# Starting the FFN behind each mixer on x times its modulation, with the RMS root applied to the products

## The chip, the cores and the metric

The kernel runs on one core of a Trainium2 chip. The metric is the device time of one execution in microseconds (us): the median of several runs. The profile is of one further execution on the chip, and its times count from the start of its span.

The engines are named as in the profile: PE (matmuls; PEld its weight loads), DVE, ACT, POOL (GpSimd) and SP. Each works through its own queue in order and waits at semaphores for the others.

## The reference

Two layers, 256 latent tokens and 256 context tokens, 1024 channels. Layer 0 mixes tokens by a 2-D Fourier transform, layer 1 by retention. A half-step FFN stands ahead of and behind each mixer, and each of them begins with an RMS norm and a modulation.

```
def rmsnorm(x, g):
    y = x * rsqrt(mean(x * x, axis=-1) + NORM_EPS)
    return y * g

def modulate(h, shift, scale):
    return h * (1 + scale) + shift

def swiglu(h, w_gate, w_up, w_down):                    # FFN_DIM = 2816
    return (silu(h @ w_gate) * (h @ w_up)) @ w_down

for l in range(2):
    def half_ffn(t, m, j):
        h = modulate(rmsnorm(t, norm_g[l, j]), m[3 * j], m[3 * j + 1])
        return t + 0.5 * m[3 * j + 2] * swiglu(h, w_gate[l, j // 2], w_up[l, j // 2], w_down[l, j // 2])
    x = half_ffn(x, m_lat, 0)
    ctx = half_ffn(ctx, m_ctx, 0)
    y_lat, y_ctx = fourier_layer(...) if l == 0 else retention_layer(...)
    x = x + m_lat[5] * y_lat                            # and ctx likewise, in layer 0
    x = half_ffn(x, m_lat, 2)                           # and ctx likewise, in layer 0
return rmsnorm(x, final_g)
```

The root of the norm is one number for each token. A matmul with the weights therefore commutes with it: W applied to (x · scale · root + shift) is (W applied to x · scale) · root + W applied to shift, with the root along the tokens and the last term one number for each output channel.

## The kernel before

Activations lie transposed: channels on the 128 partitions (eight tiles, d or k = 0 to 7), tokens in the free dimension, 256 latent columns first and 256 context columns behind them. `xlat` and `xctx` are the residual streams.

**Products.** An fp32 product is made of three fp32r matmuls (`mm3`): high part by high part (L132), high weight by the activation's low part (L133), low weight by the high part (L134). A weight block arrives raw by SP's DMA queue; ACT rounds its high part (L89, `wh`), DVE subtracts to get the low part (L90, `wl`), in pieces of 128x1024. The activations are split the same way: `h` tiles come in pairs, high and low.

**The FFN.** The 2816 hidden channels are 22 blocks of 128, each with a gate and an up product over the eight tiles k; `hidden` then applies Silu (ACT), multiplies (DVE) and splits the result. Block b needs two pieces of weights. The first blocks of each FFN are issued by a special beginning, `begin_two` (512 columns: the latent columns of two blocks first, then their context columns) or `begin_narrow` (256 columns; in the last FFN only the latent stream is left).

**Between a mixer and the FFN.** The mixer's output projection ends per tile d in a residual on DVE (`residual`, L395) and a square on ACT (L307); the squares are added up over d by POOL or DVE (`square`, L314). The last two squares of each stream are left apart (`apart=2`), so that PE sums three tiles. `rstd` then sums over the partitions with PE (L329, one column for each 128 tokens), takes the root (ACT L334, DVE L336), spreads it to a diagonal (L338) and to a row on all partitions (PE L345). `norm_mod` makes the `h` tiles: DVE x · scale · row (L361), ACT the shift and the high part (L362), DVE the low part (L363). Only then can the FFN's first product run. In the meantime `keep_warm` issues matmuls of a constant (L250) whose result nobody uses: 6, 5 and 5 of them.

This happens twice: behind Fourier (`prepare(0, 2, T2, True)`, then `begin_two`) and behind retention (`prepare(1, 2, S, True)`, then `begin_narrow`). The context's norm (`late`) is made while PE multiplies the first latent blocks. `nxt["done"]` holds the norm's operations, and `behind(d)` puts what is issued in it behind the norm of tile d.

**Order.** Each engine's order is set when the kernel is built, by a scheduler that simulates the program; `tc.issue_after` only adds an edge to it. SP's queue of weight loads runs ahead as far as its buffers go (three raw tiles, six pairs of pieces).

In Fourier, `rstd_tokens` computes the root of the mixer's own norm in another form: sums over the partitions for both streams (L384), root (L389) and reciprocal (L391) with tokens on the partitions. DVE and ACT use it in the first Fourier stages.

Of the kernel before, what the change touches and what calls it, by code (L numbers as in the profile page):

```python
# [10 lines left out]
F32 = mybir.dt.float32  # L11
# [5 lines left out]
P = 128  # L17
# [14 lines left out]
GRID_W = 64  # L32


@with_exitstack
def hybrid_block(ctx: ExitStack, tc: tile.TileContext, a: dict, out: bass.AP):
# [44 lines left out]
    def h_tile():  # L81
        return hpool.tile([P, 512], F32R, tag="h", name=nm("h"))
# [176 lines left out]
    sums = {}  # L259

# [43 lines left out]
    def square(d, s, eng=nc.gpsimd, apart=0):  # L304

        sq = q_tile()
        nc.scalar.activation(sq, x_tile(d, s), AF.Square)  # L307
# [45 lines left out]
    def norm_mod(l, j, s, h, r):  # L353
        sl = STREAMS[s]
        done, acts = [], []
        for d in range(ND):
# [3 lines left out]
            with tc.issue_after(done[d - 3].ins) if d > 2 else nullcontext():  # L360
                nc.vector.scalar_tensor_tensor(u, x_tile(d, s), sc, r, ALU.mult, ALU.mult)  # L361
# [16 lines left out]
    def rstd_tokens():  # L378

        ps = aux_tile()  # L380
        for s in range(2):
# [6 lines left out]
        root = spool.tile([P, 4], F32, tag="root4", bufs=1, name=nm("root"))  # L388
        mark[2] = nc.scalar.activation(root, ps[:, :4], AF.Sqrt, bias=epst[:, 1:2])  # L389
        inv = spool.tile([P, 4], F32, tag="inv4", bufs=1, name=nm("inv"))  # L390
# [64 lines left out]
    def half_ffn(l, j, h, width, begin, after, each=None):  # L455
        f = 2 * l + j // 2
        off = 0
        for c0, c1 in CHUNKS:
            hid = []

            def hidden(psg, psu):
                sg = t_tile()
                mark[1] = nc.scalar.activation(sg[:, :width], psg[:, :width], AF.Silu)  # L463
                hf = t_tile()
                nc.vector.tensor_tensor(hf[:, :width], psu[:, :width], sg[:, :width], ALU.mult)  # L465
                uh, ul = a_tile(), a_tile()
                split(uh[:, :width], ul[:, :width], hf[:, :width])
                hid.append((uh, ul))
# [124 lines left out]
    def fourier(l, slot, after):  # L593
# [84 lines left out]
        four["last"] = mark[0], mark[6]  # L678

        for b in range(4):  # L680
# [5 lines left out]
            for d in (2 * b, 2 * b + 1):  # L686
# [49 lines left out]
    def retention(l, slot, h, mid, after):  # L736
# [220 lines left out]
        def project_out(hd, zt, between=None, behind=None):  # L957
            for half in range(2):
                blk = wblock(a["ret_out"][slot, hd, half], 2048)
                for dd in range(4):  # L960
# [7 lines left out]
                    if hd == HEADS - 1:  # L968
                        square(d, 0, nc.vector, 2)
# [4 lines left out]
        for hd in range(HEADS):  # L974
# [55 lines left out]
    def prepare(l, j, width, warm=False):  # L1030
# [16 lines left out]
        return after  # L1047

# [96 lines left out]
    def begin_narrow(load, bank, part, hidden):  # L1145
# [134 lines left out]
```

## Time and profile before

| | us |
|---|---|
| runs | 1652.84, 1654.86, 1654.74 |
| median | 1654.74 |
| profiled execution | 1655.55 |
| its span | 1653.7 |
| Fourier's output projection ends on PE | 439.76 |
| first product of FFN (0,2) | 446.81 |
| retention's output projection ends on PE | 1447.61 |
| first product of FFN (1,2) | 1453.66 |

The profiled execution lies 0.81 us above the median. The timeline lists each engine's instructions with their start and duration; instructions alike that follow each other are drawn together (x4), and what ended an idle time stands in brackets. A window's row gives its length, then each engine's busy time in it, the clock granted to PE as a share of full speed, and the DMA engines' share. A duration in the timeline includes the time in which an instruction drains, so that the next may start before it ends; what one costs in a row of them is the distance between starts.

### The profile page before, as it was taken

What the parts mean: (1) busy time and instruction counts of PE and PEld (TensorE: products, weight loads), DVE (VectorE), ACT (ScalarE), POOL (GpSimd) and SP (SyncE); (2) the same over time, 40 slices, a digit from 0 to 9 for tenths busy, and PEclk for the clock granted to TensorE, in tenths of its full rate; (3) what the DMA queues carried; (4) which work ended last, traced back from release to release, by engine and by line L of the source; (5) the groups of instructions that cost most, each with busy time, mean ns of one, the idle gap of its engine ahead of it and who ended that gap; (6) DMA issues with size and microseconds to landing.
All of it is one profiled execution on the core that took longest, in us unless ns stands there. A gap on an engine that the chain in (4) does not pass through costs nothing.

```text
span 1653.7 us, 23197 instructions
## 1 busy us (share of the span) xinstructions
PE 1632.7 (99%) x9310; PEld 1427.1 (86%) x9310; DVE 1128.3 (68%) x1813; ACT 624.3 (38%) x912; POOL 123.6 (7%) x194
## 2 busy tenths in 40 slices
PE   7999999999999999999999999999999999999998
PEld 5888888888988888888988888888988999999998
DVE  5688888887866776766567767733666757665554
ACT  4422322346543122233442232223564454354443
POOL 0010111113200000001200000001100000000000
PEclk9999999999999999999999999999999999999999
DMA  9675776752244544544144444522133333345451
GB/s 370 225 265 183 265 259 221 252 188 77 77 142 177 178 164 165 192 158 175 52 165 170 166 164 156 191 88 100 63 128 128 128 119 137 129 169 187 166 190 53
DMA packets 59516, 272.03 MB, mean 164 GB/s; under 512 B 7409, under 2 KB 8705, under 8 KB 41745
## 3 DMA queue, kind: packets, MB, share of 16 engines
q1 hardware_dynamic: 40224, 201.76, 34.5%
q0 software_dynamic: 18640, 68.26, 11.7%
q8 instruction: 73, 1.20, 0.3%
q10 hardware_dynamic: 544, 0.52, 0.1%
q14 instruction: 35, 0.28, 0.0%
HBM read 265.27 MB, written 5.24 MB: 164 GB/s over the span
## 4 chain that ended last, share of the span: by engine, by line
PE 96%; DVE 2%; ACT 1%; issue 0%; DMA 0%; DVEq 0%; ACTq 0%
PE ps L132 31%; PE ps L133 31%; PE ps L134 31%; PE ps L790 0%; PE aux L195 0%; PE aux L250 0%; PE aux L329 0%; DVE t L269 0%; PE aux L345 0%; PE aux L951 0%; PE ps L865 0%; DVE a L90 0%; DVE xlat L395 0%; ACT wh L89 0%; DVE a L628 0%
## 5 line engine op out<-in xcount | busy, mean ns | idle before, releaser
L89 ACT CAST wh<-raw 128x1024 fp32r<-128x1024 f32 x344 | 352.3, 1031 | 709.6 <-PE ps L133 608.5
L133 PE MATMUL ps<-h,wh 128*128 128x512 f32 (+1 forms) x1568 | 556.0, 356 | 0.5 <-DVE h L1081 0.5
L134 PE MATMUL ps<-h,wl 128*128 128x512 f32 (+1 forms) x1568 | 554.8, 355 | 0.0
L132 PE MATMUL ps<-h,wh 128*128 128x512 f32 (+1 forms) x1568 | 549.3, 357 | 3.4 <-ACT h L1080 3.1
L90 DVE TENSOR_TENSOR wl<-raw,wh 128x1024 fp32r<-128x1024 f32 x344 | 410.3, 1198 | 179.2 <-ACT wh L89 176.0
L132 PEld LDWEIGHTS ps<-h,wh 128*128 128x128 f32 x1568 | 294.3, 190 | 46.1 <-ACT h L1080 4.0
L133 PEld LDWEIGHTS ps<-h,wh 128*128 128x128 f32 x1568 | 297.1, 190 | 42.6 <-DVE h L1081 1.0
L134 PEld LDWEIGHTS ps<-h,wl 128*128 128x128 f32 x1568 | 296.9, 190 | 41.6 <-DVE wl L90 0.3
L222 DVE CUSTOM_DVE_ANT_0 dump<-araw,wide,adab 128x1024 bf16<-128x1024 f32 x256 | 329.7, 1288 | 3.2
L132 PE MATMUL ps<-a,wh 128*128 128x512 f32 (+2 forms) x952 | 317.8, 337 | 0.0
L134 PE MATMUL ps<-a,wl 128*128 128x512 f32 (+2 forms) x952 | 317.7, 336 | 0.0
L133 PE MATMUL ps<-a,wh 128*128 128x512 f32 (+2 forms) x952 | 317.6, 336 | 0.0
L133 PEld LDWEIGHTS ps<-a,wh 128*128 128x128 f32 x952 | 180.9, 190 | 18.7
L134 PEld LDWEIGHTS ps<-a,wl 128*128 128x128 f32 x952 | 180.8, 190 | 18.4
L132 PEld LDWEIGHTS ps<-a,wh 128*128 128x128 f32 x952 | 180.0, 190 | 18.5
L465 DVE TENSOR_TENSOR t<-ps,t 128x512 f32<-128x512 f32 (+1 forms) x88 | 55.0, 625 | 171.3 <-PE ps L134 140.7
L213 POOL DMA_DIRECT2D araw<-in_ada_w x128 | 67.8, 530 | 819.3 <-DVE mods L222 760.1
L395 DVE SCALAR_TENSOR_TENSOR xlat<-ps,mods,xlat 128x256 f32<-128x256 f32 x128 | 61.1, 481 | 63.5 <-PE ps L134 62.9
L463 ACT ACTIVATE t<-ps 128x512 f32<-128x512 f32 (+1 forms) x88 | 47.9, 544 | 127.9 <-PE ps L134 122.5
L90 DVE TENSOR_TENSOR a<-t,a 128x512 fp32r<-128x512 f32 (+2 forms) x116 | 70.0, 607 | 2.6 <-ACT a L89 2.2
L89 ACT CAST a<-t 128x512 fp32r<-128x512 f32 (+2 forms) x116 | 64.3, 558 | 14.0 <-DVE t L894 9.8
L314 POOL TENSOR_TENSOR q<-q,q 128x256 f32<-128x256 f32 x52 | 47.1, 922 | 178.8 <-ACT q L307 178.3
(216 smaller groups left out, 1150.0 us busy)
## 6 DMA issues: line engine op xcount, KB each, us to landing
raw<-in_wgu SPq DMA_DIRECT2D x85, 1024.0 KB, 4.8
araw<-in_ada_w POOLq DMA_DIRECT2D x128, 512.0 KB, 3.8
raw<-in_wd SPq DMA_DIRECT2D x32, 896.0 KB, 4.5
raw<-in_ret_in SPq DMA_DIRECT2D x24, 1024.0 KB, 4.8
raw<-in_wd SPq DMA_DIRECT2D x16, 1024.0 KB, 4.8
a<-in_ada_first SPq DMA_DIRECT2D x32, 256.0 KB, 6.0
t<-in_four_w SPq DMA_DIRECT2D x32, 256.0 KB, 5.1
raw<-in_ret_out SPq DMA_DIRECT2D x8, 1024.0 KB, 4.7
```

Source lines behind the costliest of these rows:

```text
L89: mark[6] = nc.scalar.copy(hi, src)
L90: i = (lo_eng or nc.vector).tensor_tensor(lo, src, f32(hi), ALU.subtract)
L132: nc.tensor.matmul(ps, lh, rh, start=start, stop=False)
L133: nc.tensor.matmul(ps, lh, rl, start=False, stop=False)
L134: mark[4] = nc.tensor.matmul(ps, ll, rh, start=False, stop=stop)
L213: nc.gpsimd.dma_start(raw, a["ada_w"][l, m, d])
L222: nc.vector.tensor_tensor_reduce(dump, raw, wide[:, v, :], 1.0, adab[:, l, m, d : d + 1], ALU.mult, ALU.add, mods[l][:, m, d, v : v + 1],)
L314: eng.tensor_tensor(n, sums[s][0], sq, ALU.add)
L395: mark[0] = nc.vector.scalar_tensor_tensor(x_tile(d, s), ps, mods[l][:, m, d, s : s + 1], x_tile(d, s), ALU.mult, ALU.add)
L463: mark[1] = nc.scalar.activation(sg[:, :width], psg[:, :width], AF.Silu)
L465: nc.vector.tensor_tensor(hf[:, :width], psu[:, :width], sg[:, :width], ALU.mult)
```

## The change

Both transitions use a new class `Ahead`. Per tile d, right behind the latent residual, `tile(d)` makes the `h` pair from x · scale alone: ACT the high part, DVE the low part. `open` has written the shift (high and low part) into the first two of the context's columns of the `h` tiles, with POOL. The first products run over 258 columns: 256 of x · scale and two of the shift. They are two blocks in `begin_two`, three in `begin_narrow`. The root is computed inside the stream of products (`roots`, at k = 5 or 4), and `evict` multiplies it into the products as they leave PSUM; the shift's product is added per channel, as ACT's bias for the gate and in DVE's multiplication for up. The context's norm later overwrites the shift's columns, and the latent norm (`norm_mod`) is still made, for the blocks that follow. No `keep_warm` is left at the two places.

The squares behind Fourier are all added by POOL, for all eight tiles; those behind retention too, instead of by DVE. Block 1's weights (and block 2's in `begin_narrow`) are cast and split behind tile 7. `rstd_tokens` gets the number of streams and goes through them in reverse; Fourier's own root uses it as well.

```
-    def rstd_tokens():
+    def rstd_tokens(n=2, scale=1.0):
         ps = aux_tile()
-        for s in range(2):
+        for s in reversed(range(n)):
             for t in range(2):
                 for i, sq in enumerate(sums[s]):
                     mark[5] = nc.tensor.matmul(
...
     def fourier(l, slot, following):
...
+        following.open()
         for b in range(4):
...
                 for s in range(2):
                     residual(d, z[:, STREAMS[s]], l, 5, s)
-                    square(d, s, nc.gpsimd, 2)
-                    if d == ND - 1 and s == 0:
-                        sqrt_table()
-                        keep_warm(NW[0], mark[4])
-                        after(0)
-        after(1)
+                    if s == 0:
+                        following.tile(d)
+                for s in (1, 0):
+                    square(d, s)
+        sqrt_table()
...
     def project_out(hd, zt, between=None, behind=None):
...
                     if hd == HEADS - 1:
-                        square(d, 0, nc.vector, 2)
+                        following.tile(d)
+                        square(d, 0)
...
+        following.open()
         project_out(HEADS - 1, zts.pop(0))
-        keep_warm(NW[0], mark[4])
-        after(0)
...
+    class Ahead:
+        def open(self):
+            need(self.l, 3 * self.j + 1)
+            nxt["h"] = self.h = h_tiles()
+            nxt["done"] = [], []
+            for d, (hi, lo) in enumerate(self.h):
+                sh = mods[self.l][:, 3 * self.j, d, 0:1].broadcast_to([P, SH])
+                hi, lo = (t[:, S : S + SH] for t in (hi, lo))
+                nc.gpsimd.tensor_copy(hi, sh)
+                nc.gpsimd.tensor_tensor(lo, sh, f32(hi), ALU.subtract)
+        def tile(self, d):
+            sc = mods[self.l][:, 3 * self.j + 1, d, 0:1]
+            hi, lo = (t[:, STREAMS[0]] for t in self.h[d])
+            nxt["done"][1].append(nc.scalar.activation(hi, x_tile(d, 0), AF.Copy, scale=sc))
+            mark[0] = nc.vector.scalar_tensor_tensor(lo, x_tile(d, 0), sc, f32(hi), ALU.mult, ALU.subtract)
+            nxt["done"][0].append(mark[0])
+        def products(self, blk, ps, k):
+            hi, lo = (t[:, : S + SH] for t in self.h[k])
+            for gu in range(2):
+                mm3(ps[gu][:, : S + SH], wcols(blk, k // 4 * 1024 + gu * 512 + k % 4 * P, P), (hi, lo), k == 0, k == ND - 1)
+        def evict(self, ps, r):
+            col = spool.tile([P, 2], F32, tag="col", name=nm("col"))
+            v = []
+            for gu in range(2):
+                nc.vector.tensor_copy(col[:, gu : gu + 1], ps[gu][:, S : S + 1])
+                v.append(q_tile())
+                nc.vector.tensor_tensor(v[gu], ps[gu][:, :S], r, ALU.mult)
+            return v, col
+        def gate(self, v, col, pair):
+            uh, ul = pair
+            sg = q_tile()
+            mark[1] = nc.scalar.activation(sg, v[0], AF.Silu, bias=col[:, 0:1])
+            hf = q_tile()
+            nc.vector.scalar_tensor_tensor(hf, v[1], col[:, 1:2], sg, ALU.add, ALU.mult)
+            split(uh[:, :S], ul[:, :S], hf)
+        def roots(self, n):
+            inv = rstd_tokens(n, 1.0 / D**2)
+            diag = t_tile()[:, : n * S]
+            nc.vector.tensor_tensor(...)
+            r = aux_tile()
+            for s in range(n):
+                self.rowed = nc.tensor.matmul(r[:, STREAMS[s]], meanw, diag[:, STREAMS[s]], start=True, stop=True)
+            row = q_tile()
+            nc.scalar.copy(row, r[:, :S])
+            return r, row
+        def begin_two(self, load, bank, part, hidden):
+            late = STREAMS[1]
+            h = self.h
+            blks, lat = [load(0)], [(bank(), bank()) for _ in range(2)]
+            with behind(ND - 1), tc.issue_after(squared[0].ins):
+                blks.append(load(1))
+            for k in range(ND):
+                self.products(blks[0], lat[0], k)
+                if k == 5:
+                    r, row = self.roots(2)
+            for k in range(ND):
+                with tc.issue_after(self.rowed.ins) if k > 3 else nullcontext():
+                    self.products(blks[1], lat[1], k)
+            nxt["done"] = norm_mod(self.l, self.j, 1, h, r[:, late])
+            with behind(3):
+                first = self.evict(lat[0], row)
+            with behind(ND - 1):
+                second = self.evict(lat[1], row)
+                pre = [load(2)]
...
+            for k in range(ND):
+                for i in range(2):
+                    for gu in range(2):
+                        part(blks[i], ctx[i][gu], gu, (k,), late)
+                if k == 0:
+                    with tc.issue_after(mark[0].ins), tc.issue_after(mark[6].ins):
+                        nxt["done"] = norm_mod(self.l, self.j, 0, h, r[:, :S])
...
```

`begin_narrow` is written in the same way, with three blocks, one stream and the latent norm into other tiles than those that the first products read.

In the new program the lines move: L90 becomes L94, L132 to L134 become L136 to L138, L314 becomes L319, L361 to L363 become L366 to L368, L384 becomes L389, L395 becomes L400, L702 to L704 become L710 to L712. New are L1077 (ACT) and L1078 (DVE) in `tile`, L1094 and L1096 in `evict`.

What stands in the engines' queues shows three places. The first is PE in the first stage of Fourier, where the sums for its own root are issued among the stage's products (`aux_3459` is the tile of sums, `q_3398` the latent's and `q_3405` the context's sum of squares). Before:

```order
L132 MATMUL ps_3480<-a_2979,h_158 128x256
L384 MATMUL aux_3459<-meanw,q_3398 128x1 x2
L133 MATMUL ps_3480<-a_2980,h_158 128x256
L134 MATMUL ps_3480<-a_2979,h_159 128x256
L132 MATMUL ps_3480<-a_2979,h_156 128x256
L384 MATMUL aux_3459<-meanw,q_3405 128x1 x2
L133 MATMUL ps_3480<-a_2980,h_156 128x256
```

And in the changed program:

```order
L136 MATMUL ps_3480<-a_2979,h_156 128x256
L137 MATMUL ps_3480<-a_2980,h_156 128x256
L138 MATMUL ps_3480<-a_2979,h_157 128x256
L136 MATMUL ps_3480<-a_2979,h_158 128x256
L137 MATMUL ps_3480<-a_2980,h_158 128x256
L389 MATMUL aux_3459<-meanw,q_3405 128x1 x2
L389 MATMUL aux_3459<-meanw,q_3398 128x1 x2
L138 MATMUL ps_3480<-a_2979,h_159 128x256
```

Both sums now stand together, the latent's behind the context's, and the last of them has four products more ahead of it than before.

The second is DVE at the end of Fourier's output projection (`t` are a tile's outputs of both streams, `h` the pairs of the next FFN, `wl` the weights' low parts of its block 1). Before, the rows from the last tile's output on:

```order
L702 TENSOR_TENSOR t_4081<-ps_4052,t_4066 128x2x128
L703 TENSOR_TENSOR t_4081<-ps_4052,t_4066 128x2x128
L704 COPY t_4081<-ps_4052 128x2
L395 SCALAR_TENSOR_TENSOR xlat<-t_4081,mods_126,xlat 128x256
L395 SCALAR_TENSOR_TENSOR xctx_98<-t_4081,mods_126,xctx_98 128x256
L336 RECIPROCAL inv_4122<-root_4120 128x2
L338 TENSOR_TENSOR q_4124<-ident,inv_4122 128x256
```

And in the changed program:

```order
L400 SCALAR_TENSOR_TENSOR xlat<-t_4131,mods_126,xlat 128x256
L400 SCALAR_TENSOR_TENSOR xctx_98<-t_4131,mods_126,xctx_98 128x256
L1078 SCALAR_TENSOR_TENSOR h_3752<-xlat,mods_126,h_3751 128x256
L1078 SCALAR_TENSOR_TENSOR h_3754<-xlat,mods_126,h_3753 128x256
L94 TENSOR_TENSOR wl_4166<-raw_4163,wh_4165 128x1024
L94 TENSOR_TENSOR wl_4170<-raw_4163,wh_4169 128x1024
L396 RECIPROCAL inv_4216<-root_4214 128x4
L1111 TENSOR_TENSOR t_4218<-ident,inv_4216 128x512
```

The low parts of tiles 6 and 7 stand behind every residual, and a pair of weight splits stands ahead of the root's reciprocal.

The third is PE in the new stream, from the last products of block 0 (`wh_4155`, k = 7) to the first of block 1 (`wh_4165`, k = 0); `q_4141` and `q_4145` are the sums of squares, each the result of the last addition for its stream:

```order
L137 MATMUL ps_4160<-h_3754,wh_4155 128x258
L138 MATMUL ps_4160<-h_3753,wl_4156 128x258
L389 MATMUL aux_4209<-meanw,q_4141 128x1 x2
L136 MATMUL ps_4161<-h_3739,wh_4165 128x258
L137 MATMUL ps_4161<-h_3740,wh_4165 128x258
L136 MATMUL ps_4162<-h_3739,wh_4165 128x258
L137 MATMUL ps_4162<-h_3740,wh_4165 128x258
L389 MATMUL aux_4209<-meanw,q_4145 128x1 x2
L138 MATMUL ps_4161<-h_3739,wl_4166 128x258
```

The sums that began the norm before now follow all of block 0's products, and the first product with block 1's low part follows the second sum.

More of the change, by code (lines that the diff above doesn't have):

```diff
@@ L734, in rsqrt_small, with retention @@
         return y
-    def retention(l, slot, h, mid, after):
+    def retention(l, slot, h, mid, following):
         need(l, NMOD - 1)
@@ L1047, in prepare, with __init__, begin_narrow @@
         return after
+    class Ahead:
+        def __init__(self, l, j):
+            self.l, self.j = l, j
+        def open(self):
[16 more added lines that the diff above has]
+            for gu in range(2):
+                mm3(
+                    ps[gu][:, : S + SH], wcols(blk, k // 4 * 1024 + gu * 512 + k % 4 * P, P), (hi, lo),
+                    k == 0, k == ND - 1,
+                )
+        def evict(self, ps, r):
[16 more added lines that the diff above has]
+            diag = t_tile()[:, : n * S]
+            nc.vector.tensor_tensor(
+                diag.rearrange("p (a b) -> p a b", b=P), ident.unsqueeze(1).broadcast_to([P, 2 * n, P]),
+                inv.unsqueeze(2).broadcast_to([P, 2 * n, P]), ALU.mult,
+            )
+            r = aux_tile()
[23 more added lines that the diff above has]
+                pre = [load(2)]
+            ctx = [(bank(), bank()) for _ in range(2)]
+            for k in range(ND):
[5 more added lines that the diff above has]
+                        nxt["done"] = norm_mod(self.l, self.j, 0, h, r[:, :S])
+            pairs = [(a_tile(), a_tile()) for _ in range(2)]
+            with behind(ND - 1):
+                self.gate(*first, pairs[0])
+                self.gate(*second, pairs[1])
+                for i in range(2):
+                    hidden(*ctx[i], pairs[i], late)
+                pre.append(load(3))
+            return 2, pre
+        def begin_narrow(self, load, bank, part, hidden):
+            n = 3
+            blks, lat = [load(0)], [(bank(), bank()) for _ in range(n)]
+            with behind(ND - 1), tc.issue_after(squared[0].ins):
+                blks += [load(i) for i in range(1, n)]
+            for k in range(ND):
+                self.products(blks[0], lat[0], k)
+                if k == 4:
+                    r, row = self.roots(1)
+            first = self.evict(lat[0], row)
+            self.h, h = self.h[:], self.h
+            h[:] = [halves_of(a_tile()) for _ in range(ND)]
+            with tc.issue_after(mark[0].ins), tc.issue_after(mark[6].ins):
+                nxt["done"] = norm_mod(self.l, self.j, 0, h, r[:, :S], slice(0, S), range(5))
+            with behind(4):
+                pre = [load(n)]
+            with tc.issue_after(mark[0].ins), tc.issue_after(mark[6].ins):
+                done = norm_mod(self.l, self.j, 0, h, r[:, :S], slice(0, S), range(5, ND))
+            nxt["done"] = tuple(i + j for i, j in zip(nxt["done"], done))
+            for i in range(1, n):
+                for k in range(ND):
+                    with tc.issue_after(self.rowed.ins) if k > 3 else nullcontext():
+                        self.products(blks[i], lat[i], k)
+            with behind(ND - 1):
+                pre.append(load(n + 1))
+                for ready in [first] + [self.evict(ps, row) for ps in lat[1:]]:
+                    pair = halves_of(a_tile())
+                    self.gate(*ready, pair)
+                    hidden(None, None, pair, None)
+            return n, pre
```

60 lines of the change are left out of this document (28 added, 32 removed).

## The prediction

> **What bounds the kernel now.** I read the page first: its busy times, and the chain that ended last.
>
> ```profile
> span 1653.7 us, 23197 instructions
> PE 1632.7 (99%) x9310; PEld 1427.1 (86%) x9310; DVE 1128.3 (68%) x1813; ACT 624.3 (38%) x912; POOL 123.6 (7%) x194
> PE 96%; DVE 2%; ACT 1%; issue 0%; DMA 0%; DVEq 0%; ACTq 0%
> ```
>
> PE carries the chain nearly throughout. But busy is not useful: 32 of its matmuls at each of two places only keep it occupied while other engines compute a norm. So the second view is PE's timeline at these places (start, duration, instruction, idle time ahead). The first, between Fourier projection and FFN, I call T1:
>
> ```profile
> 439.52 0.28 PE L133 MATMUL ps<-a,wh 128*128 128x258 f32 x1
> 439.64 0.28 PE L134 MATMUL ps<-a,wl 128*128 128x258 f32 x1
> 439.76 1.50 PE L250 MATMUL aux<-meanw 128*128 128x128 f32 x12
> ...
> 445.93 1.02 PE L329 MATMUL aux<-meanw,q 128*128 128x1 f32 x8
> 446.81 0.49 PE L132 MATMUL ps<-h,wh 128*128 128x256 f32 x2
> 447.14 0.28 PE L133 MATMUL ps<-h,wh 128*128 128x256 f32 x1
> 447.26 0.28 PE L134 MATMUL ps<-h,wl 128*128 128x256 f32 x1
> ```
>
> From 439.76 to 446.81 no product of the FFN runs: **7.05 us**. The first two products then take 0.33 us instead of 0.24, a loss of 0.09. The rows also give the price of a product: starts lie 0.12 us apart with 258 columns (439.52, 439.64) and with 256 (447.14, 447.26). T2, behind retention:
>
> ```profile
> 1447.49 0.28 PE L134 MATMUL ps<-a,wl 128*128 128x256 f32 x1
> 1447.61 1.50 PE L250 MATMUL aux<-meanw 128*128 128x128 f32 x12
> 1449.30 1.47 PE L329 MATMUL aux<-meanw,q 128*128 128x1 f32 x12 [0.19 <-DVE q L314]
> ...
> 1453.66 0.74 PE L132 MATMUL ps<-h,wh 128*128 128x256 f32 x4
> ...
> 1455.12 0.52 PE L132 MATMUL ps<-h,wh 128*128 128x256 f32 x3
> ```
>
> From 1447.61 to 1453.66: **6.05 us**. Ten products then take 1.46 us instead of 1.20: 0.26 more.
>
> **The change part by part: what it removes.** The first products now need only x times its scale, so PE can go from the last projection product into the FFN. What remains of the norm on PE stands inside the product stream. Its price there is in the chain of waits (time on the chain, count; each fp32 matmul is recorded twice):
>
> ```profile
> 449.46 0.34 PE aux L329 x4
> 453.50 0.43 PE aux L345 x2
> ```
>
> At T1 the context's last sum (0.34) and row (0.43) stood in the stream already. Now there are four sums (x8: 0.68) and two rows (0.86), 1.54 against 0.77. At T2 there are two sums and one row, 0.77 against nothing outside the gap. Removed: T1 7.05 + 0.09 + 0.77 − 1.54 = 6.37; T2 6.05 + 0.26 − 0.77 = 5.54; **together 11.91 us**. Two more columns cost nothing by the 0.12 pitch; at most 2/256 of 11.5 us of products at T1 and 17.3 at T2, 0.2 us.
>
> **What it adds at T1.** DVE gets eight operations L1078 between the residuals, two of them behind all residuals in the order above. GpSimd gets four more squares' additions (14 instead of 10). Both meet at this stage:
>
> ```profile
> 429.03 2.35 DVE L90 TENSOR_TENSOR wl<-raw,wh 128x1024 fp32r<-128x1024 f32 x2
> 432.02 0.93 DVE L395 SCALAR_TENSOR_TENSOR xlat<-t,mods,xlat 128x256 f32<-128x256 f32 x1
> 432.88 0.96 DVE L395 SCALAR_TENSOR_TENSOR xctx<-t,mods,xctx 128x256 f32<-128x256 f32 x1
> ...
> 438.12 0.41 DVE L702 TENSOR_TENSOR t<-ps,t 128x256 f32<-128x256 f32 x1
> 438.45 0.41 DVE L703 TENSOR_TENSOR t<-ps,t 128x256 f32<-128x256 f32 x1
> ...
> 441.17 0.49 DVE L395 SCALAR_TENSOR_TENSOR xlat<-t,mods,xlat 128x256 f32<-128x256 f32 x1
> 441.57 0.48 DVE L395 SCALAR_TENSOR_TENSOR xctx<-t,mods,xctx 128x256 f32<-128x256 f32 x1
> 429.51 6.51 POOL L314 TENSOR_TENSOR q<-q,q 128x256 f32<-128x256 f32 x6 [35.63 <-ACT q L307]
> 436.28 3.31 POOL L314 TENSOR_TENSOR q<-q,q 128x256 f32<-128x256 f32 x4 [0.27 <-ACT q L307]
> 432.00:442.00 10.00, 10.00 (x86) 9.96 (x85) 9.70 (x21) 4.42 (x12) 7.21 (x9) 1.00 0.30 105
> ```
>
> While GpSimd adds, a DVE operation with two SBUF inputs starts 0.86 us after the one before (432.02, 432.88); alone 0.40 (441.17, 441.57). So each addition puts about 0.47 us into DVE's queue. The last row (busy PE, PEld, DVE, ACT, POOL in ten us) leaves DVE 0.3 us idle; ACT at 4.42 has room for eight more scalings.
>
> The last residual before ends at 441.57 + 0.40 = 441.97. Eight L1078 at 0.395 add 3.2, four additions 1.9; idle time gives back 0.3, and the last two additions fall behind tile 7, onto the weight split (−0.9). Tile 7 is then ready at about 445.8; PE wants it at 439.76 + 42 × 0.12 = 444.80. It waits about 1.1 us for tiles 6 and 7, and some 0.4 more for the last addition's sum. **T1's stalls: 1.5 us.** Below, no contention gives 0 (445.1 less the idle time). Above, an operation that always costs 0.86 puts tile 7 at 449 (rival B). I take the middle because the additions are counted there.
>
> Block 1's split of the weights waits behind tile 7. Behind it on DVE stand the root, the context's norm, the evictions, block 2's split, the latent norm:
>
> ```profile
> 451.50 2.36 DVE L90 TENSOR_TENSOR wl<-raw,wh 128x1024 fp32r<-128x1024 f32 x2
> 453.97 1.26 DVE L361 SCALAR_TENSOR_TENSOR q<-xctx,mods,aux 128x256 f32<-128x256 f32 x3
> ...
> 460.27 2.36 DVE L90 TENSOR_TENSOR wl<-raw,wh 128x1024 fp32r<-128x1024 f32 x2
> 470.96 0.23 PE ps L132
> ```
>
> A split pair takes 2.3 us, sixteen norm operations 6.3 (453.97 to 460.27). That is 2.3 + 0.9 + 6.3 + 2.0 (eight copies and scalings of the evictions at 0.25 on average, an estimate between the residual's 0.40 and a short copy) + 2.3 + 6.3 = 20.1 us behind tile 7, until about 466. Block 2 begins now at 470.96, 24 us after the first product; in the new order at about 439.76 + 24.1 + 0.8 + 1.5 = 466, and uses tile k only 0.7 us × k later. The latent norm is done by then: 0, and up to 2 us if DVE falls behind.
>
> **What it adds at T2.** Here PE waits for nothing of the projection:
>
> ```profile
> 1447.81 0.48 DVE L395 SCALAR_TENSOR_TENSOR xlat<-ps,mods,xlat 128x256 f32<-128x256 f32 x1 [0.39 <-PE ps L134]
> 1459.30 4.63 DVE L90 TENSOR_TENSOR wl<-raw,wh 128x1024 fp32r<-128x1024 f32 x4 [0.33 <-ACT wh L89]
> ```
>
> The last residual is at 1447.81. With a scaling on ACT and L1078 behind it, tile 7 is there at about 1449.5; PE wants it at 1447.61 + 42 × 0.12 = 1452.65. The squares, now GpSimd's, have until 1451. Later splits (1.15 us each) wait behind evictions; placed by hand one of block 4 comes 0.3 us late. I take **0.3**, between 0 and one split.
>
> **What moves in Fourier.** The root of Fourier's own norm is computed by the same function, whose loop is now reversed, and its sums stand four products later on PE. There DVE, not PE, is the bound:
>
> ```profile
> 396.34 0.35 PE aux L384 x4
> ...
> 411.96 0.39 PE L134 MATMUL ps<-a,t 128*128 128x256 f32 x1 [0.81 <-DVE t L90]
> ```
>
> The chain goes through L384 into DVE's work, and PE still waits for DVE at 411.96. Four products at 0.12 make **0.48 us** (0 if DVE's work has slack, 0.6 at most). The 16 small shift writes on GpSimd fall into the 35.63 us in which it was idle (the row of 429.51). DVE is packed there; 0, at most 0.8 if eight subtractions each hold a DVE operation up by 0.1.
>
> **The sum:** 11.91 − 1.5 − 0.3 − 0.48 = 9.6 us. The profiled execution took 1655.55 us (span 1653.7), so 1645.9 on its scale; it lies 0.8 above the median of 1654.74, so **1645.1**.
>
> [...] The gate on PE's clock (last but one column of the windows) fell once after short waits:
>
> ```profile
> 1189.77 0.66 PE L865 MATMUL ps<-a,h 128*128 128x128 f32 x4 [0.92 <-ACT ht L870]
> 1191.00:1192.00 1.00, 1.00 (x5) 0.81 (x4) 1.00 (x3) 1.00 (x4) 0.00 (x0) 0.71 0.00 0
> 1192.00:1193.00 1.00, 1.00 (x4) 0.81 (x3) 0.82 (x3) 1.00 (x3) 0.00 (x0) 0.50 0.55 115
> 1193.00:1194.00 1.00, 1.00 (x3) 0.74 (x3) 1.00 (x2) 1.00 (x2) 0.00 (x0) 0.50 0.94 360
> 1194.00:1195.00 1.00, 1.00 (x4) 0.80 (x3) 1.00 (x2) 1.00 (x2) 0.00 (x0) 0.58 0.97 410
> ```
>
> The lost clock is 0.29 + 0.50 + 0.50 + 0.42 = 1.7 us. The same after T1's stalls would give 1646.8, inside the forecast's own range. [...]
>
> **The rivals.**
> B, GpSimd holds DVE off longer: every two-input operation costs 0.86. Tile 7 comes at 449 and PE is idle for 4.2 us, which drops the clock (1.7). Against it: DVE runs at 0.40 where no addition is in flight. Gain 11.91 − 4.5 − 0.3 − 0.48 − 1.7 = 4.9: 1649.8. [...]
> C, as B, and the clock falls at T2 too: gain 3.2, 1651.5, no difference to measure (±0.2% is 3.3 us, what a measurement here can tell from none).
> D, slower: DVE and GpSimd exclude each other for whole recorded durations, 0.48 + 0.83 per pair. Fourteen pairs from 432 on (18.3), three operations alone (1.2), eight reads of PSUM at 0.33 (438.12, 438.45) and five short copies (3.6 together) put tile 7 at about 455. PE then waits 10.3 us, at the sums and splits behind it 2.7 more, and the clock falls: −11.9 + 13.0 + 0.8 + 1.7 = 3.6 slower, 1658.3. It decides from tile 7 later than about 452, where the stalls reach 9.4 us. The 0.86 speaks against it.
> That the change doesn't do what it says is excluded for PE's order: no L250 stands at the two places any more.
>
> **How the numbers follow.** Forecast (1642.6 to 1648) 0.68; B 0.15; C 0.07; D 0.06; better than 1642.6, were there no stalls, 0.04. The range leaves out C, D and the better case: 1642.6 to 1651. Faster 0.68 + 0.15 + 0.04 = 0.87, same 0.07, slower 0.06.
>
> **What would show it.** Right: at T1 the first product of 258 columns 0.12 us behind the last projection product; waits of PE for L1078 and the sums of about 1.5 us together, granted clock 1.00; at T2 no wait before 1460; Fourier's end 0.5 us later. Wrong: L1078 of tile 7 more than 2 us behind PE's need (B, D), a clock of 0.50 (C), or PE waiting for the norm in block 2.

## The result, and the profile after

| | median, us | range | runs |
|---|---|---|---|
| before | 1653.79 | 1651.89 to 1654.86 | 4 |
| changed | 1644.32 | 1643.48 to 1646.88 | 4 |

The ratio is 0.9948, with a 95% interval of 0.9936 to 0.9959: 6.8 to 10.6 us faster. The forecast was 1645.1. It was counted from 1654.74, the median of three executions; a fourth, at 1651.89, moves that median to 1653.79.

The changed kernel's page, its span, busy times and the chain:

```profile
span 1642.0 us, 23175 instructions
PE 1619.2 (99%) x9222; PEld 1414.5 (86%) x9222; DVE 1138.5 (69%) x1846; ACT 630.4 (38%) x933; POOL 141.8 (9%) x237
PE 94%; DVE 2%; DMA 2%; ACT 1%; issue 0%; SPq 0%; POOL 0%; DVEq 0%; ACTq 0%; POOLq 0%
```

PE is still 99% busy; its busy time fell by 13.5 us and DVE's rose by 10. The page doesn't tell where the gain is. PE's timeline does. T1 in the changed kernel, from the last product of Fourier's projection to the first product of 512 columns:

```profile
439.38 0.28 PE L138 MATMUL ps<-a,wl 128*128 128x258 f32 x1
439.50 0.28 PE L136 MATMUL ps<-h,wh 128*128 128x258 f32 x1
...
443.82 0.40 PE L136 MATMUL ps<-h,wh 128*128 128x258 f32 x2
444.93 0.36 PE L137 MATMUL ps<-h,wh 128*128 128x258 f32 x1 [0.71 <-DVE h L1078]
...
446.36 0.55 PE L389 MATMUL aux<-meanw,q 128*128 128x1 f32 x4
446.77 0.37 PE L136 MATMUL ps<-h,wh 128*128 128x258 f32 x1
...
447.97 0.61 PE L389 MATMUL aux<-meanw,q 128*128 128x1 f32 x4 [0.47 <-POOL q L319]
...
466.17 0.63 PE L136 MATMUL ps<-h,wh 128*128 128x512 f32 x2
```

The FFN's first product follows 0.12 us behind the projection's last. There are two waits: for L1078 (tile 6's low part) 0.87 us by the starts, and at the second sum 0.63. From 439.50 to 466.17 it takes 26.67 us. Before, the first product of 512 columns started at

```profile
470.80 0.40 PE L132 MATMUL ps<-h,wh 128*128 128x512 f32 x1
```

which is 31.04 us behind 439.76. T1 gained 4.37 us. T2 in the changed kernel has no gap and no wait:

```profile
1441.04 0.28 PE L138 MATMUL ps<-a,wl 128*128 128x256 f32 x1
1441.15 0.28 PE L136 MATMUL ps<-h,wh 128*128 128x258 f32 x1
```

To compare whole profiles I cut them at starts of PE instructions that every kernel has: the first product ahead of Fourier (L567 before, at 350.97), the projection's end (439.76), retention's first product (L790, 1173.25), its last transpose (L951, near 1434.9), the last keep_warm of the final norm (L250, 1648.46), and the span's end. In us:

| kernel | to 351 | Fourier | T1 and on | retention | T2 and on | output |
|---|---|---|---|---|---|---|
| before | 350.97 h | 88.79 h | 733.49 | 261.66 h | 213.55 | 5.28 |
| changed | 350.21 | 89.29 h | 729.12 | 259.83 | 208.24 | 5.27 |
| changed_again | 351.25 h | 89.30 h | 729.17 | 259.81 | 208.23 | 5.27 |
| changed_third | 351.20 h | 89.29 h | 729.18 | 259.83 | 208.23 | 5.28 |
| t1_only | 349.66 | 89.30 h | 729.24 | 259.83 | 213.54 | 6.68 |
| t2_only | 350.38 | 87.34 | 733.46 | 260.05 | 208.24 | 5.28 |
| fourier_forward | 351.44 h | 87.37 | 729.14 | 261.49 h | 208.23 | 5.28 |
| no_additions | 351.17 h | 89.25 h | 727.29 | 261.31 h | 208.23 | 5.27 |
| squares_dve | 351.36 h | 89.26 h | 729.95 h | 259.88 | 208.23 | 5.29 |
| squares_dve_forward | 351.03 h | 88.78 h | 729.96 h | 260.08 | 208.23 | 5.26 |
| before_no_warm | 349.80 | 88.38 h | 734.55 h | 260.20 | 216.88 h | 5.27 |
| tile_first | 350.88 h | 88.81 h | 729.68 | 259.88 | 208.24 | 5.27 |
| apart1 | 351.48 h | 89.33 h | 728.82 | 259.89 | 208.23 | 5.28 |
| apart1_forward | 349.76 | 87.36 | 728.83 | 261.53 h | 208.23 | 5.27 |

An h marks a stretch in which PE's granted clock fell to 0.50 for 3.4 us (in before_no_warm for 6.8 us at T1 and 10.2 at T2). Without one, the stretches of Fourier, T1 and T2 repeat within 0.12 us where the code is the same, even between kernels; retention then spreads over 0.4 us, and the start over 0.7. So the change is worth 733.49 − 729.12 = 4.37 us at T1 and 213.55 − 208.24 = 5.31 at T2, and costs 89.29 − 88.79 = 0.50 in Fourier (both with an h): **9.18 us**, beside 9.47 by the medians. The profiled spans differ by 11.7; the remaining 2.6 are the h stretches at the start and in retention, which the profile of before has and that of the changed kernel hasn't.

### The profile page after: what moved, and what is told of

It is laid out like the page before. It is cut to its first block, busy times and chain, and to the rows that moved or that the text cites. A ratio compares the mean times of both kernels' runs of the same rounds, so it can differ in the third digit from the quotient of the medians.

```text
span 1642.0 us, 23175 instructions
## 1 busy us (share of the span) xinstructions
PE 1619.2 (99%) x9222; PEld 1414.5 (86%) x9222; DVE 1138.5 (69%) x1846; ACT 630.4 (38%) x933; POOL 141.8 (9%) x237
## 3 DMA queue, kind: packets, MB, share of 16 engines
HBM read 265.27 MB, written 5.24 MB: 165 GB/s over the span
## 4 chain that ended last, share of the span: by engine, by line
PE 94%; DVE 2%; DMA 2%; ACT 1%; issue 0%; SPq 0%; POOL 0%; DVEq 0%; ACTq 0%; POOLq 0%
PE ps L137 31%; PE ps L136 31%; PE ps L138 31%; DMA a<-in_ada_first 2%; PE ps L797 0%; DVE wl L94 0%; PE ps L872 0%; ACT wh L93 0%; PE aux L199 0%; DVE xlat L400 0%; PE aux L958 0%; SPq L147 0%; DVE h L1078 0%; DVE a L94 0%; DVE xctx L400 0%
## 5 line engine op out<-in xcount | busy, mean ns | idle before, releaser
L94 DVE TENSOR_TENSOR wl<-raw,wh 128x1024 fp32r<-128x1024 f32 x344 | 410.9, 1202 | 164.2 <-ACT wh L93 160.8
L137 PE MATMUL ps<-h,wh 128*128 128x512 f32 (+2 forms) x1264 | 469.1, 372 | 1.2 <-DVE h L1078 0.7
L138 PE MATMUL ps<-h,wl 128*128 128x512 f32 (+2 forms) x1264 | 468.5, 372 | 0.0
L136 PE MATMUL ps<-h,wh 128*128 128x512 f32 (+2 forms) x1264 | 463.1, 373 | 3.6 <-ACT h L1220 3.1
L137 PE MATMUL ps<-a,wh 128*128 128x256 f32 (+2 forms) x1256 | 403.3, 323 | 0.0
L136 PE MATMUL ps<-a,wh 128*128 128x256 f32 (+2 forms) x1256 | 403.2, 324 | 0.0
L138 PE MATMUL ps<-a,wl 128*128 128x256 f32 (+2 forms) x1256 | 402.7, 323 | 0.0
L136 PEld LDWEIGHTS ps<-h,wh 128*128 128x128 f32 x1264 | 235.7, 188 | 46.3 <-ACT h L1220 4.0
L137 PEld LDWEIGHTS ps<-h,wh 128*128 128x128 f32 x1264 | 237.9, 188 | 43.2 <-DVE h L1221 1.0
L138 PEld LDWEIGHTS ps<-h,wl 128*128 128x128 f32 x1264 | 237.7, 188 | 41.3 <-DVE wl L94 0.3
L137 PEld LDWEIGHTS ps<-a,wh 128*128 128x128 f32 x1256 | 239.1, 191 | 18.5
L138 PEld LDWEIGHTS ps<-a,wl 128*128 128x128 f32 x1256 | 238.7, 191 | 18.3
L136 PEld LDWEIGHTS ps<-a,wh 128*128 128x128 f32 x1256 | 238.1, 191 | 18.8
L400 DVE SCALAR_TENSOR_TENSOR xlat<-ps,mods,xlat 128x256 f32<-128x256 f32 x128 | 61.2, 481 | 64.9 <-PE ps L138 64.3
L319 POOL TENSOR_TENSOR q<-q,q 128x256 f32<-128x256 f32 x63 | 57.3, 924 | 212.6 <-ACT q L312 208.8
L94 DVE TENSOR_TENSOR a<-t,a 128x512 fp32r<-128x512 f32 (+2 forms) x113 | 68.1, 608 | 2.4 <-ACT a L93 2.0
```

The source lines that it names most:

```text
L94: i = (lo_eng or nc.vector).tensor_tensor(lo, src, f32(hi), ALU.subtract)
L136: nc.tensor.matmul(ps, lh, rh, start=start, stop=False)
L137: nc.tensor.matmul(ps, lh, rl, start=False, stop=False)
L138: mark[4] = nc.tensor.matmul(ps, ll, rh, start=False, stop=stop)
L319: eng.tensor_tensor(n, sums[s][0], sq, ALU.add)
L400: mark[0] = nc.vector.scalar_tensor_tensor(x_tile(d, s), ps, mods[l][:, m, d, s : s + 1], x_tile(d, s), ALU.mult, ALU.add)
```

## The experiments

**One transition alone.** t1_only puts T2 back, t2_only T1 and Fourier's order of sums. In t1_only:

```
-                        following.tile(d)
-                        square(d, 0)
+                        square(d, 0, nc.vector, 2)
...
-        following.open()
         project_out(HEADS - 1, zts.pop(0))
+        keep_warm(NW[0], mark[4])
+        following(0)
...
-    following = Ahead(1, 2)
-    retention(1, 0, nxt["h"], late, following)
-    half_ffn(1, 2, nxt["h"], S, following.begin_narrow, finish, scale_out)
+    retention(1, 0, nxt["h"], late, prepare(1, 2, S, True))
+    half_ffn(1, 2, nxt["h"], S, begin_narrow, finish, scale_out)
```

> The changed kernel, with the transition behind retention put back as it was before (keep_warm, norm, two blocks of 256 columns). Theory, the two transitions add up: the stretch from the end of Fourier's projection on PE to the first product of 512 columns is 26.7 us as in the changed kernel (31.0 before), T2's gap is 6.0 us again, Fourier costs 0.5; 4.37 - 0.5 = 3.9 us faster than before. Rival, the changed kernel's gain hangs on the clock or on run-to-run differences elsewhere: the stretch is 26.7 us and the time still not 3 to 5 us below before.

Measured: 1651.62 us against 1653.91 before on the same chip, ratio 0.9987 (0.9978 to 0.9996): 2.3 us, not 3.9. By the time alone that is the rival's sign, a gain of less than 3 us. The stretches are as the theory has them (729.24 at T1, 213.54 at T2). What is missing stands in the output, 6.68 us instead of 5.28. The DMA issues on ACT's queue, in t1_only:

```profile
1642.42 2.79 ACTq L1312 DMA_DIRECT2D out<-a  x2
```

and before:

```profile
1649.03 1.57 ACTq L1172 DMA_DIRECT2D out<-a  x2
```

The two issues take 1.2 us longer and start 0.3 us later behind the same work. This is one profile, and why is not settled. It lies at the kernel's end, behind both transitions, so the rival falls by the stretches.

In t2_only:

```
-        following.open()
...
-                    if s == 0:
-                        following.tile(d)
-                for s in (1, 0):
-                    square(d, s)
-        sqrt_table()
+                    square(d, s, nc.gpsimd, 2)
+                    if d == ND - 1 and s == 0:
+                        sqrt_table()
+                        keep_warm(NW[0], mark[4])
+                        following(0)
+        following(1)
...
-    following = Ahead(0, 2)
-    fourier(0, 0, following)
-    half_ffn(0, 2, nxt["h"], T2, following.begin_two, prepare(1, 0, T2))
+    fourier(0, 0, prepare(0, 2, T2, True))
+    half_ffn(0, 2, nxt["h"], T2, begin_two, prepare(1, 0, T2))
```

> The changed kernel, with the transition behind Fourier put back as it was before and Fourier's own sums in the old order. Theory: 5.3 us faster than before, all of it behind 1440 us, and nothing moved ahead of that. Together with the kernel that has only the first transition changed the gains make the changed kernel's 9.5. Rival, T2's gain came in part from the first transition (a clock or a queue that was shifted): under 4 us.

Measured: 1648.97 us against 1653.91, ratio 0.9964 (0.9951 to 0.9976): 4.9 us, and 208.24 in T2's stretch, 733.46 in T1's. By the stretches the theory holds: each transition gains about what it does in the changed kernel (4.25 and 5.31), and neither moves the other. By the medians the two make 7.2 us and not 9.5; 1.4 of the rest is t1_only's output, and what remains is inside the intervals.

**Fourier's order of sums.**

```
-        for s in reversed(range(n)):
+        for s in (range(n) if scale == 1.0 else reversed(range(n))):
```

> The changed kernel, with the loop over the streams forward again where the function serves Fourier's own root; the sums of the FFN's root stay reversed. Theory, the sums stand on the path into DVE's packed work: PE's last sum (L389) for it comes 0.4 to 0.5 us earlier, and Fourier's projection ends 0.5 us earlier, counted from the same point ahead of Fourier; time 0.5 lower than the changed kernel, at the edge of what five rounds show. Rival, DVE has slack or the clock takes it back: the sums come earlier and the projection's end does not move.

Measured: 1643.39 us, ratio to before 0.9938 (0.9924 to 0.9951), and 87.37 us for Fourier instead of 89.29. That is 1.9 us and not 0.5, since this profile has no half clock there. Windows of four us (length; busy PE, PEld, DVE, ACT, POOL; granted clock, the third figure from the end of such a row; the DMA engines' share and GB/s), in the changed kernel:

```profile
408.00:412.00 4.00, 2.11 (x13) 1.49 (x13) 3.83 (x16) 3.24 (x13) 0.00 (x0) 1.00 0.01 2
412.00:416.00 4.00, 3.96 (x21) 3.75 (x21) 2.44 (x10) 1.36 (x5) 0.00 (x0) 0.57 0.02 4
```

and in fourier_forward:

```profile
408.00:412.00 4.00, 2.56 (x18) 1.95 (x16) 3.83 (x17) 3.45 (x13) 0.00 (x0) 1.00 0.01 4
412.00:416.00 4.00, 3.49 (x26) 3.26 (x27) 3.25 (x14) 1.86 (x8) 0.00 (x0) 1.00 0.00 0
```

PE waits for DVE in the first window of both; only in one does the clock fall behind it. Like with like, both with a half clock: squares_dve_forward and tile_first, which keep the old order, take 88.78 and 88.81; all seven profiles with the reversed loop 89.25 to 89.33. (before_no_warm, the old order too, takes 88.38: its half clock begins 60.7 us into the stretch, the others' at 62.2 to 63.1.) The last of the sums starts 45.46 us into the stretch in fourier_forward and 45.95 in the changed kernel. The order costs 0.5 us, as the theory has it. Those seven all show the half clock, of the seven with the old order four; whether the order also makes it likelier stays open.

**GpSimd's additions behind Fourier.**

```
                 for s in (1, 0):
-                    square(d, s)
+                    square(d, s, apart=ND)
+                    sums[s] = sums[s][-1:]
```

> The changed kernel without the 14 additions of squares behind Fourier: the root is computed from the squares of tile 7 alone; everything else, the order on DVE too, is as in the changed kernel. Theory, the additions take DVE's time by contention: the two-input operations there cost 0.40 throughout, L1078 of tile 7 ends 1.5 us or more earlier, PE's wait of 0.9 for L1078 and of 0.6 at the sums both go, 1.2 to 1.5 us faster than the changed kernel. Rival, the eight operations L1078 are too many for DVE in any case: the wait for L1078 stays near 0.9 us, and only the one at the sums goes (0.6).

The kernel leaves out the additions, so its norm isn't the reference's. Measured: 727.29 us in T1's stretch against 729.12 to 729.18, 1.85 us less; the median 1642.04. PE waits for nothing between 436 and 465. On DVE in the changed kernel and GpSimd beside it:

```profile
437.27 0.96 DVE L400 SCALAR_TENSOR_TENSOR xctx<-t,mods,xctx 128x256 f32<-128x256 f32 x1
438.15 0.47 DVE L400 SCALAR_TENSOR_TENSOR xlat<-t,mods,xlat 128x256 f32<-128x256 f32 x1
438.55 0.47 DVE L400 SCALAR_TENSOR_TENSOR xctx<-t,mods,xctx 128x256 f32<-128x256 f32 x1
...
443.83 1.83 DVE L1078 SCALAR_TENSOR_TENSOR h<-xlat,mods,h 128x256 fp32r<-128x256 f32 x2
445.72 3.28 DVE L94 TENSOR_TENSOR wl<-raw,wh 128x1024 fp32r<-128x1024 f32 x2
443.58 4.34 POOL L319 TENSOR_TENSOR q<-q,q 128x256 f32<-128x256 f32 x4 [1.33 <-ACT q L312]
```

and in no_additions:

```profile
443.14 0.88 DVE L1079 SCALAR_TENSOR_TENSOR h<-xlat,mods,h 128x256 fp32r<-128x256 f32 x2
445.01 2.36 DVE L94 TENSOR_TENSOR wl<-raw,wh 128x1024 fp32r<-128x1024 f32 x2 [0.99 <-ACT wh L93]
```

While four additions run (443.58 to 447.92), the pair L1078 takes 1.83 us instead of 0.88 and the pair of splits 3.28 instead of 2.36. Tile 7 is ready 6.16 us behind the projection's end (445.66 − 439.50), without additions 3.60 (444.02 − 440.42). The rival, too many operations for DVE in any case, falls: without additions PE doesn't wait. Up to tile 7 nine of DVE's operations with two SBUF inputs last 0.41 to 0.54 us longer than alone, 4.2 us together. Without additions DVE idles for 1.5 us there, so tile 7 comes only 2.56 us earlier.

**The additions on DVE.**

```
-                    square(d, s)
+                    square(d, s, nc.vector)
```

> The changed kernel with the 14 additions of squares behind Fourier on DVE instead of GpSimd. Theory, contention: alone an addition costs DVE 0.33 us, while one on GpSimd held DVE up by about 0.47. The last residual before ended at 441.97; minus ten times 0.47, plus eight L1078 (3.2) and twelve additions (4.0) makes tile 7 ready at about 444.4, just when PE wants it, and no operation there takes 0.86: PE's waits for L1078 and at the sums shrink from 1.85 us with their restarts to under 0.5, 1.3 to 1.8 us faster than the changed kernel from the end of the projection to retention. Rival, DVE has no room for 14 more operations: tile 7 comes later than now (444.9) and the stretch grows by 1 us or more.

Measured: 729.95 us in T1's stretch, 0.8 more than in the changed kernel. PE's waits and, in windows of four us, its clock:

```profile
PE ps L137 <- DVE h L1078: 0.4, 1, 0.4
PE ps L136 <- ACT h L1077: 0.3, 1, 0.3
```

```profile
444.00:448.00 4.00, 3.27 (x27) 2.92 (x25) 4.00 (x11) 2.54 (x5) 0.00 (x0) 1.00 0.00 0
448.00:452.00 4.00, 4.00 (x22) 4.00 (x23) 2.69 (x4) 0.73 (x2) 0.00 (x0) 0.57 0.26 49
```

The waits at the sums are gone, but tile 7 comes 6.27 us behind the projection's end, as late as with GpSimd's additions, where I had worked out 4.6. Twelve additions at 0.33 take 4.0 us of DVE's time ahead of tile 7. On GpSimd the same twelve cost it 4.2: those that met an operation with two SBUF inputs cost it 0.4 to 0.5, those that met a read of PSUM or a short copy nothing (L710 and L711 start 0.33 us apart beside the addition at 438.88, and at 435.26 with none). In the kernel before the ten additions made DVE's operations 2.9 us longer by its trace, where I had taken off ten times 0.47, 4.7 us. That is the step that failed here. The rival, no room on DVE, is nearer: DVE idles for only 0.25 us up to tile 7, though the stretch grew by 0.8 and not by 1. The clock then falls to half from 448 to 451.5, a loss of 0.43 × 4 = 1.7 us. Without that the stretch would be near 728.2, an estimate. The median, 1643.21, can't be told from the changed kernel's.

> The same, with Fourier's own sums in the old order too. If both effects stand by themselves: Fourier's stretch 0.5 us shorter and T1's 1.3 to 1.8 shorter than in the changed kernel, 2 us together, faster than both kernels. If Fourier's order only moved the clock's half-speed stretch, then T1's part alone.

Measured: 88.78 and 729.96 us, 1643.99 by the median. Fourier's part stands by itself; at T1 the half clock comes again, and the 2 us together are not there.

**A version without keep_warm.** Before, the calls are taken out, and the two `prepare` lose their `True`:

```
-                        keep_warm(NW[0], mark[4])
...
-        keep_warm(NW[0], mark[4])
```

> The kernel before, without the keep_warm matmuls at the two places (those at the end stay); PE waits there instead. Theory of the forecast (no fall of the clock in T1 or T2 for about 1.5 us of waiting, but unknown for more): the gaps of 7.05 and 6.05 us stay within 0.3 us, since DVE and ACT set them. If PE's clock falls after a wait of some microseconds, 1.7 us are lost behind each gap, up to 3.4 us slower; a clock of 0.50 for three windows then stands behind 447 and 1454.

Measured: 1656.89 us against 1654.44, ratio 1.0017 (1.0008 to 1.0026): 2.4 us slower. The clock, in windows of two us:

```profile
442.00:444.00 2.00, 1.68 (x6) 1.51 (x7) 0.62 (x2) 0.00 (x0) 0.00 (x0) 0.50 0.00 0
444.00:446.00 2.00, 2.00 (x10) 2.00 (x11) 2.00 (x6) 1.58 (x4) 0.00 (x0) 0.50 0.00 0
...
1450.00:1452.00 2.00, 1.19 (x2) 0.50 (x2) 0.62 (x3) 0.00 (x0) 0.00 (x0) 0.50 0.00 0
...
1456.00:1458.00 2.00, 2.00 (x12) 2.00 (x11) 1.97 (x5) 1.69 (x3) 0.00 (x0) 0.50 0.00 0
```

So keep_warm did its work: without it the clock falls at both places, T1's stretch is 1.06 us longer and T2's 3.33 (one profile). The gaps, expected within 0.3 us of 7.05 and 6.05, are 6.72 us at T1 (438.18 to 444.90) and 7.03 at T2 (1445.63 to 1452.66), and the first products behind both run at half clock. That part of the theory falls. The changed kernel does without these matmuls because it has products in their place (its clock stays at 1.00 from 436 to 468 us and from 1436 to 1460), not because they were needless.

> The changed kernel again, on the same chip as the other three and with another profile. Theory: the stretches between Fourier's end and retention, and behind retention, repeat within 0.1 us; the stretches with a clock of 0.50 (near 17, 413 and 1190 us) come and go from execution to execution, and differences of 1.5 us or more between profiles lie there alone. Rival, they belong to the kernel: this profile shows them at the places where the first one does (413 only).

Measured: 729.17 and 208.23 us, within 0.05 of the first profile. This profile has a half clock near 18 us that the first one lacks. It goes with the execution, not with the kernel.

**Where PE's wait lies.** tile_first has fourier_forward's edit, and:

```
                 for s in range(2):
-                    residual(d, z[:, STREAMS[s]], l, 5, s)
+                    with tc.issue_after(mark[0].ins) if s and d > 5 else nullcontext():
+                        residual(d, z[:, STREAMS[s]], l, 5, s)
```

> The changed kernel with Fourier's own sums in the old order, and at T1 L1078 of tiles 6 and 7 ahead of the context residuals of the same tiles on DVE. Nothing is taken from DVE or GpSimd. Theory, DVE's queue up to the sums and block 1's first split is the bound, not one instruction's place in it: PE's wait of 0.87 us for L1078 goes or halves, and comes back at the sums or at block 1's split; the stretch from the projection's end to retention stays within 0.4 us of 729.1. Rival, the order is what costs: the wait goes for good, the stretch shrinks by 0.9 us or more.

Measured (one execution, 1644.54 us): 729.68 us at T1, 0.5 more than the changed kernel. PE's waits between 436 and 465:

```profile
PE aux L389 <- POOL q L319: 1.9, 2, 1.4
```

The figures are the total in us, the number of waits and the longest. The wait for L1078 is gone and a longer one stands at the sums: their additions come later, since the context residuals do. The stretch grew by a little more than the 0.4 I had allowed; the rival, 0.9 shorter, falls. A place in DVE's order moves the wait, it doesn't remove it.

**Fewer additions, more sums.**

```
-                    square(d, s)
+                    square(d, s, nc.gpsimd, 1)
```

> The changed kernel with the last square of each stream left apart: 12 additions on GpSimd instead of 14, and four more sums on PE (8 records at 0.11, 0.9 us). Theory: the two additions taken away are the ones behind tile 6 and 7, so the wait at the sums (0.6) goes and PE pays 0.9 for it: the stretch from the projection's end to retention is 0 to 0.5 us longer than 729.1. Rival, additions cost more than the sums: 0.5 us or more shorter.

Measured (one execution, 1644.81 us): 728.82 us at T1, 0.3 less, between what the two expected. What is left:

```profile
PE aux L389 <- POOL q L319: 0.4, 1, 0.4
```

By this list the wait for L1078 goes and 0.4 stays at the sums, the other way than I had it. The timeline shows why:

```profile
445.17 1.83 DVE L1078 SCALAR_TENSOR_TENSOR h<-xlat,mods,h 128x256 fp32r<-128x256 f32 x2
445.89 0.38 PE L389 MATMUL aux<-meanw,q 128*128 128x1 f32 x2 [0.36 <-POOL q L319]
446.18 0.39 PE L137 MATMUL ps<-h,wh 128*128 128x258 f32 x1
```

DVE's last tiles come no earlier: tile 7 is ready at 447.00, 6.19 us behind the projection's end (440.81), against 6.16. But one of the sums (two records) now stands ahead of the first product that reads tile 6's low part, so PE waits for this sum and works on it in the time in which it waited for L1078 alone. The last sums, which need no addition behind tile 7 any more, don't wait.

**Both edits.** apart1_forward has apart1's edit and fourier_forward's.

> The last square of each stream left apart, and Fourier's own sums in the old order: the two edits that shortened a stretch by themselves (0.3 and 0.5 us). If they add up, the stretch from 351 us to the projection's end is 88.8 us with a stretch of half clock near 413 or 87.4 without one, that from there to retention 728.8, and the time is about 0.8 us below the changed kernel's on the same chip, less than five rounds can tell for sure. Rival: without the delay in Fourier the clock or the waits at T1 take it back.

> The changed kernel on the same chip, to compare with: 1643 to 1647 in single executions, the stretches as before (89.3, 729.1, 208.2) apart from those with a clock of 0.50.

Measured: 1643.09 us (1642.08 to 1647.43) and 1645.11 (1643.40 to 1645.35) on the same chip, ratios to before 0.9940 (0.9927 to 0.9952) and 0.9943 (0.9930 to 0.9955). The stretches are as expected, 87.36 and 728.83 against 89.29 and 729.18. If Fourier's stretch is taken at 88.8, as other kernels with the old order have it with a half clock, the kernel with both edits is 0.85 us better, an estimate; by the time the two can't be told apart.

## Why the prediction was right

**What the change removes** was right at both places: the first product follows the last one in 0.12 us, no L250 is left there, and at T2 PE waits for nothing. At T2 the forecast was 5.54 − 0.3 = 5.24 and the stretch gained 5.31. No split came late, so the 0.3 was not paid. Of the 0.23 that 5.31 lacks to 5.54, the products' distance makes up half: their starts lie 0.1208 us apart on average (1441 to 1458), against 0.1200 in the kernel before; for 144 of them that is 0.12 us. The two more columns alone don't explain it, since at T1 products of the same 258 columns start 0.1200 apart; the cause stays open. I had put this at nothing, with 0.2 as its end.

**T1** was forecast at 6.37 − 1.5 = 4.87 and gained 4.37. The stalls came at their places, and their sum is right: 0.87 for L1078 and 0.63 at the sums, 1.5 together, where I had 1.1 and 0.4. Tile 7 was ready 6.16 us behind the projection's end, where I had 6.04 (445.8 − 439.76). The missing 0.5 are two smaller terms. Behind the waits and the sums the next products start more slowly, by 0.07 us five times (444.93 to 445.12 in place of 0.12), and the sums and rows in the stream took 0.41 + 0.47 for the sums (446.36 to 446.77, 447.97 to 448.44) and 0.86 for the rows, 1.74 instead of 1.54. That the additions cause both waits is shown by no_additions (1.85 us less, no wait). The price of 0.47 for each of them is not: it holds where an addition meets an operation with two SBUF inputs, and not every one does. By the traces the additions ahead of the last tile cost DVE 2.9 us before (ten) and 4.2 in the changed kernel (twelve), 0.29 and 0.35 for one. The forecast needed only the difference. It had 1.9 − 0.9 = 1.0 us for it, and 1.3 was measured: the price was too high on both sides, and most of that cancels. So tile 7's place came out well in part by luck; where the price counted in full, in squares_dve, it failed by 1.7 us.

**Fourier's root**, 0.48: measured 0.50, by stretches with the same clock.

**The latent norm** is in time: block 2 starts at 466.17, forecast 466, and waits for nothing.

**The rivals.** B, DVE held off in every operation, falls: rows at 0.88 (437.27 to 438.15) and at 0.40 (438.15 to 438.55) stand side by side. An addition lasts 0.73 us where it meets reads of PSUM only (438.88) and up to 1.06 beside operations with two SBUF inputs (439.62), yet DVE's next operation starts 0.88 behind the one before, and not 0.40 + 0.73 = 1.13 or more, as it would if one waited for the whole of the other. The clock at T1 did not fall in the changed kernel's three profiles, with waits of 1.2 us by the list of PE's waits (1.5 by the starts); but in the two profiles with the additions on DVE it did, with waits of 0.7 by the list; in tile_first, with 1.9, it did not. So the case that I put inside the forecast's own range was near. The forecast had read one such fall from the profile before; its trace has three, at 17.25, 413.19 and 1191.43 us, the second 1.2 us behind the end of the wait at 411.96 that the forecast shows. D, exclusion for whole durations (its 0.83 is a quarter of the 3.31 us at 436.28 in the profile before), falls with B.

**The time** came out at 1644.32 against 1645.1, but the forecast was counted from a median 0.95 higher, so the gains are to be compared: 9.6 forecast, 9.18 by stretches. The difference is T1's 0.5, and T2's 0.07 the other way. That the medians give 9.47, closer still, is luck: they hold some of the clock's chance.

## What to carry to other kernels

A per-token factor that commutes with a matmul lets the next layer start before the factor is known; what it gains is the whole stretch in which the matmul engine was kept busy with nothing, less what its producers then make it wait for. Such a gain is read from the gap, the stall from the queue of the engine that makes the operands, counted instruction by instruction up to the last tile. When differences of a few us are compared, cut the profiles at common instructions and compare stretches with the same granted clock. At T1, where the stretch repeated within 0.12 us, 0.3 us could be told so; by the medians of five runs not 1 us.

## What the runs showed of the hardware that was not expected

PE's clock falls to half for about 3.4 us at the same few places (near 18, 413 and 1190 us) in some executions and not in others of the same code, and each time costs 1 to 1.7 us: Fourier with the old order takes 88.38 to 88.81 us with a fall and 87.34 to 87.37 without. In retention, four of fourteen profiles have it: 261.3 to 261.7 us against 259.8 to 260.2. The windows before and behind, in the kernel before:

```profile
1186.00:1190.00 4.00, 3.08 (x28) 2.94 (x27) 4.00 (x10) 3.67 (x6) 0.00 (x0) 1.00 0.00 0
1190.00:1194.00 4.00, 3.78 (x13) 2.97 (x13) 3.82 (x7) 4.00 (x9) 0.00 (x0) 0.68 0.37 119
```

and at the same work in the changed kernel:

```profile
1182.00:1186.00 4.00, 2.89 (x24) 2.61 (x23) 4.00 (x9) 3.78 (x7) 0.00 (x0) 1.00 0.00 0
1186.00:1190.00 4.00, 3.97 (x17) 3.30 (x18) 3.82 (x7) 4.00 (x7) 0.00 (x0) 1.00 0.49 178
```

PE is idle for 0.9 us in one and 1.1 in the other, and it is the first that loses its clock. How much is idle in such a window doesn't decide it alone.

The traces show what goes with it. Windows of one us (in changed_third of four) place the changes of the granted clock in eleven of the profiles. In each of them all changes ahead of the output lie whole steps of 3.413 us apart (before: 17.25, 20.66, 413.19, 416.60, 1191.43 and 1194.84 us), and these steps lie differently over the same code in each execution. In t2_only, which falls in the output alone, they are counted back from there (1642.02). Where retention's first product starts 2.30 to 3.33 us into a step, the clock falls in retention (before, fourier_forward and no_additions); where it starts 0.20 to 1.79 into one, it doesn't (the other eight). So there the moment goes with the fall; no run set it. At T1 the two profiles with the additions on DVE have nearly the same moment (the projection ends 2.26 and 2.29 into a step), and no profile of the changed kernel has it (2.78 to 3.02): whether the additions' place or the moment dropped the clock there stays open.

The falls go with a good part of the 3 to 5 us by which single executions of one kernel differ: of the kernel before, beside t1_only, the fastest (1651.22 us) had a mean clock of 1.000 and the slowest (1656.26) one of 0.996.

An addition on GpSimd cost DVE on average about as much time as the same addition on DVE (0.35 and 0.33 us). Moving such work from one to the other gained nothing here; only leaving it out did.
